# A two-layer hybrid backbone step: warm-up, early sum of squares and the last output in three parts

## The chip, the cores and the metric

The kernel runs on one core of a Trainium2 chip. The metric is the device time of one execution in microseconds (us), median of several runs.

The core has a matrix engine (TensorE, PE in the profile; its weight loads are listed as PEld), a vector engine (VectorE, DVE), a scalar engine (ScalarE, ACT), GpSimd (POOL) and a queue engine (SyncE, SP) that issues nearly all transfers here. TensorE's products land in PSUM, eight banks of 512 fp32 columns by 128 partitions.

## The reference

One inference step of two layers over 640 tokens (512 latent, 128 context) of width 1024. A layer does

```python
h = rms_norm(x, norm_g) * (1.0 + scale) + shift    # shift, scale, gate = silu(cond) @ ada_w[l] + ada_b[l]
u = h @ w_in[l]                                    # one wide input projection, cut into 16 parts
# four head groups on u: differential attention (A), gated convolution (B),
# latent attention (C), 2-D neighbourhood attention (D)
y = concat(group * silu(its gate path)) @ w_out[l]
x = x + gate * y
```

and a final RMSNorm with a gain follows the second layer. The modulation (`shift`, `scale`, `gate`) is one vector for the latent and one for the context tokens. The outputs are the final x and the context's keys and values of both layers. All arithmetic is fp32 accuracy: a large product is formed as three fp32r products of split operands (high x high, high x low, low x high).

## The kernel before

The activations stand transposed in the local memory, features on the 128 partitions, in eight feature blocks; tokens are columns, latent tokens 0 to 512, context 512 to 640. Every matrix operand is split into a high half, made by ScalarE as a rounded copy (`whi`, `hh`), and a low half, made by VectorE as the difference (`wlo`, `hl`).

The order of the work isn't the order of the code. The code records operations in a plan (`R`, an object of `Plan`), each with a priority: its place in the code, plus `R.offset`, plus a shift of its group from the table `SHIFT`. `Plan.schedule` then plays the machine through with prices from `Plan.price` and puts each engine's operations into one list; of those that can start, the one with the lowest priority goes first. In `Plan.price` an fp32r matmul costs 0.4375 ns for each moving column and 6 ns, and `schedule` lets one matmul start at the earliest 58 ns behind another (line 407). Each engine executes its list strictly in order. All operations are issued through one line of the program, so rows of the profile are told apart by tile names, not by lines.

The start of the kernel (lines 516 to 631, 847 to 875): the tokens of the first part (0 to 384, `START`) come by eight transfers into `cst`. The modulation weights of the first layer's first eight blocks come as 16 transfers of 512 KB (`adaw`), two for each block; `ada_first` multiplies each half by the condition vectors (`cs`), four matmuls that fill one PSUM bank in four strips, and derives `modB` and `modA`. The second part of the tokens (384 to 640) comes behind the fifth of these transfers (`X1`), and the four weight pieces of the first projection ("a") are put between them at the places of `WA`. `keep_warm` (line 544) lets TensorE multiply a matrix of ones by itself, 15 times ahead of everything and then 10, 8, 4 and 4 times behind the first four half blocks (`WARM`); these products are used by nobody. One fp32 matmul appears as two records in the trace. `rms_rows` (line 671) squares the eight feature blocks of a token part on ScalarE, adds them on VectorE, sums over partitions with one matmul by ones, and takes logarithm and exponential for the reciprocal root. `finish` (line 690) multiplies by the root, applies `modA` and `modB` and splits. Then the first projection runs (`tm_chunk`, 120 matmuls with 512 moving columns).

The end of a layer (lines 1313 to 1368): the output projection goes over token parts (`HALVES`), and within a part over eight feature blocks `fb`; a block is 24 matmuls (eight feature blocks, three products) with a 128 x 128 piece of `w_out` as the stationary operand and the part's tokens as the moving one. VectorE then adds gate times product to the old x (one instruction for latent and one for context tokens, where a part has both). Behind a part's eighth block, in the second layer, comes the final norm of that part: `rms_rows`, eight scalings by the gain, two multiplications by the root (each for four feature blocks) and two stores. The last part's sum of squares takes the eighth block in a matmul of its own (cuts 0, 7, 8). The second part's old x is fetched by one transfer into `xall`.

Of the kernel before, what the change touches and what calls it, by code (L numbers as in the profile page):

```python
# [20 lines left out]

L = 2
X1 = (4, 4, 4, 4, 4, 4, 4, 4)
WA = (2, 6, 11, 16)
LATE = (16, 17)
HALVES = (((0, 384), (384, 640)), ((0, 384), (384, 640)))
START = ((0, 384), (384, 640))
RMS = ((0, 8), (0, 8))
YK = (0, 1, 4, 5, 2, 6, 3, 7)
# [3 lines left out]
SWAP = 1290  # L33
SILU = 8
SLOW, LATER = 1.1, 800
WARM = (15, 10, 8, 4, 4)
SHIFT = {"": 38, "a0": 47, "a1": -28, "ada0": -8588, "av0": 6296, "av1": 3, "b0": 25951, "b1": 24557, "c0": -2462, "d0": 62, "d1": 33941, "f0.0": -174, "f0.1": 22, "f1.0": -183, "f1.1": 2841, "h0.0": -4317, "h0.1": 205, "h1.0": 7, "h1.1": -10499, "h10.0": 1418, "h10.1": -8, "h11.0": 638, "h11.1": 4686, "h2.0": -3351, "h2.1": -22079, "h3.0": -2855, "h4.0": -2974, "h4.1": -2909, "h5.0": -1, "h5.1": -9, "h6.0": 797, "h6.1": -6113, "h7.0": 20, "h7.1": 13278, "h8.0": 5300, "h9.0": -7596, "lam": 6901, "o0.0": -505, "o1.0": -80, "o1.1": 26, "p0.0": 162, "p0.1": -20, "p2.0": -2125, "p2.1": 432, "p3.0": -1337, "p3.1": 4371, "p4.0": -1388, "p4.1": -27369, "p7.0": -1727, "p7.1": 960, "p8.1": -18800, "pa0": 51, "pa1": -552, "qk00": -18970, "qk01": 10605, "qk10": 10903, "qk11": 14623, "x0": -3000, "x1": 6892, "x2": -1536, "y0": -1625, "y1": 9425, "y2": -77, "z0": -13, "z1": -227}
FILL = (('z', 4), ('d', 6), ('qk0', 7), ('qk1', 8), ('b', 12))
D = 1024
NT = 640  # L40
# [442 lines left out]
def body(ctx: ExitStack, tc: tile.TileContext, i, o):  # L483
# [12 lines left out]
    R = Plan()  # L496
    V, S, PE, SP = (R.engine(e) for e in ("DVE", "ACT", "PE", "SP"))

    def mmtile():
        return R.tile([128, 512], F32, tag="mm", space="psum")  # L500
# [41 lines left out]
    warm = mmtile()  # L542

    def keep_warm(n, after=None):
        for _ in range(n):
            PE.matmul(warm[:, 0:128], ones, ones, start=True, stop=True)
            if after is not None:
                R.ops[-1].deps.add(after)
                R.ops[-1].prio += 10 ** 6
                R.ops[-1].cost = {"PE": 215}  # L550
    keep_warm(WARM[0])
    for op in R.ops[-WARM[0]:]:
        op.cost = {"PE": 320}

    modA = R.tile([128, L, 8, 2], F32, name="modA")
    modB = R.tile([128, L, 8, 2], F32, name="modB")
# [1 line left out]
    b1 = R.tile([128, L, 8], F32, name="b1")  # L558
# [11 lines left out]
    def wpiece(l, name, idx):  # L570
        if l == 0 and name == "a":
            at(WA[idx])
            R.offset += WBOOST
        else:
            R.offset = 0
        off, kk, n = PIECES[name][idx]
        src = i["win"][l, off:off + 128 * kk * n].rearrange("(p c) -> p c", p=128)
        return wsplit(src, kk, n)

    def wsplit(src, kk, n, place=None):  # L580
        raw = R.tile([128, 1024], F32, name="wraw", tag="wraw", bufs=3)
# [13 lines left out]
    def at(h):  # L595

        R.offset = ada_at[min(h, 15)] + 7.5 * max(h - 15, 0) + 0.5 - len(R.ops)

    def ada_rows(l, blk, raws, warm):
        pa = (ttile if warm else mmtile)()  # L600
        for hf, raw in enumerate(raws):
            for k in range(4):
                PE.matmul(pa[32 * k:32 * k + 32, 0:256], cs[:, 4 * hf + k, :], raw[:, 256 * k:256 * k + 256],
                          start=(hf == 0), stop=(hf == 1))
            if warm and 2 * blk + hf < 4:
                keep_warm(WARM[1 + 2 * blk + hf], len(R.ops) - 1)
        sb = R.tile([128, 256], F32, name="adasb", bufs=1)
        S.activation(sb, pa[:, 0:256], AF.Copy)
        return sb

    def ada_first(l, blk, places):

        for hf in range(2):
            ada_at.append(len(R.ops))
            SP.dma_start(places[hf], i["adaw"][l, blk, hf])
        sb = ada_rows(l, blk, places, True)
        pb = ttile()
        for c in range(2):
            PE.matmul(pb[:, 2 * c:2 * c + 2], sb[:, 128 * c:128 * c + 128], sel, start=True, stop=True)
        R.need = len(R.ops) - 1  # L620
        V.tensor_scalar(modB[:, l, blk], pb[:, 0:2], sp[:, l, blk:blk + 1], None, op0=OP.add)
        V.tensor_scalar(modA[:, l, blk], pb[:, 2:4], b1[:, l, blk:blk + 1],
                        sp[:, l, 24 + blk:25 + blk], op0=OP.add, op1=OP.mult)

    def ada_block(l, blk):

# [209 lines left out]
    for l in range(L):  # L836
        if l == 0:
            flat = [(R.tile([128, 8, NT], F32, name="yt").rearrange("p a b -> p (a b)"), 5),
                    (R.tile([128, 6, 768], F32, name="adst").rearrange("p a b -> p (a b)"), 4),
                    (R.tile([128, 1280], F32, name="qs", bufs=2), 1),  # L840
                    (R.tile([128, 1280], F32, name="qs", bufs=2), 1),
                    (R.tile([128, 1536], F32, name="ks", bufs=2), 1),
                    (R.tile([128, 1536], F32, name="ks", bufs=2), 1),
                    (R.tile([128, BIAS_W], F32, name="bias"), 1),
                    (R.tile([128, 2816], F32, name="hl"), 2)]
            places = [t[:, 1024 * k:1024 * (k + 1)] for t, n in flat for k in range(n)]
            for blk in range(8):
                ada_first(0, blk, places[2 * blk:2 * blk + 2])
            R.need = None
            for kt in range(8):  # L850
                at(X1[kt])
                SP.dma_start(x_cur[1][:, kt], i["xt"][kt, :, START[0][1]:])
            R.begun = len(R.ops) - 1
            par = R.tile([128, P_W], F32, name="par")
            at(LATE[0])
            SP.dma_start(par, i["params"])
            ident, bones = par[:, 0:128], par[:, 128:256]
            rope = par[:, 256:512].rearrange("p (t c) -> p t c", t=4)
            fg = par[:, 512:520]
            lamt = R.tile([128, NT], F32, name="osb", bufs=2)[:, :L * 128].rearrange("p (l a c) -> p l a c", l=L, a=4)  # L860
            at(LATE[1])
            SP.dma_start(lamt, i["lam"].rearrange("l a c -> (l a c)").partition_broadcast(128)
                              .rearrange("p (l a c) -> p l a c", l=L, a=4))
            R.offset = 0
            rstds = []
            for n, x in enumerate(x_cur):
                R.group = f"x{n}"
                first = len(R.ops)
                rstds.append(rms_rows(x, RMS[n], n == 0))
                for op in R.ops[first:]:  # L870
                    op.deps.add(table)
            for kt in range(8):
                for n, (x, c, rstd) in enumerate(zip(x_cur, START, rstds)):
                    R.group = f"{'xy'[n]}{min(kt, 2)}"
                    finish(0, x, kt, *c, rstd)
            R.group = "lam"
            bonesr = R.tile([128, 128], F32R, name="bonesr")
            S.activation(bonesr, bones, AF.Copy)
            neglam = R.tile([128, L], F32, name="neglam")
            lprod = R.tile([128, NT], F32, name="osb", bufs=2)[:, :L * 64].rearrange("p (l a c) -> p l a c", l=L, a=2)  # L880
            for a in range(L):
                V.tensor_mul(lprod[:, a], lamt[:, a, 0:4:2, :], lamt[:, a, 1:4:2, :])
            V.tensor_reduce(lsum, lprod, AX.X, OP.add)
            S.activation(lsum, lsum, AF.Exp)
            V.tensor_sub(neglam, lsum[:, :, 1], lsum[:, :, 0])
            ga = R.tile([128, L], F32, name="ga")
            for a in range(L):
                li = 0.8 - 0.6 * math.exp(-0.3 * a)
                V.tensor_scalar(neglam[:, a:a + 1], neglam[:, a:a + 1], -li, None, op0=OP.add)
                V.tensor_scalar(ga[:, a:a + 1], sp[:, a, 32:33], 1.0 - li, None, op0=OP.mult)  # L890
            R.group = ""
# [425 lines left out]
        cstt = R.tile([128, 6 * C_W], F32, name="cst", tag="cst")  # L1317
        xns = halves(cstt, HALVES[l])
        wo = []
# [4 lines left out]
                    R.tile([128, 1024], F32R, name="wk", tag="ks", bufs=2)) for n in range(2)]  # L1324
        big2 = R.tile([128, 4, 1024], F32R, name="wyt", tag="yt")
        places += [(big2[:, 2 * n], big2[:, 2 * n + 1]) for n in range(2)]
        c0, c1 = HALVES[l][1]
        xall = R.tile([128, 2816], F32, name="xall", tag="hl")[:, :8 * (c1 - c0)].rearrange("p (k c) -> p k c", k=8)
        SP.dma_start(xall, xsrc[:, :, c0:c1].rearrange("k p c -> p k c"))
        for hf, (c0, c1) in enumerate(HALVES[l]):  # L1330
            R.group = f"o{hf}.{l}"
            xn = xns[hf]
            for fb in range(8):
# [3 lines left out]
                wh, wl = wo[fb]  # L1337
                w = c1 - c0
                if hf:
                    xo = xall[:, fb]  # L1340
                else:
                    xo = R.tile([128, NT], F32, name="xo", tag=("osb", "q3")[fb % 2], bufs=(2, 4)[fb % 2])
                    SP.dma_start(xo[:, :w], xsrc[fb, :, c0:c1])
# [11 lines left out]
                if l + 1 < L:  # L1355
                    SP.dma_start(xdram[fb, :, c0:c1], xn[:, fb])
            R.group = f"f{hf}.{l}"
            rstd = rms_rows(xn, (0, 7, 8) if l + 1 == L and hf == 1 else (0, 8))
            if l + 1 < L:
                for kt in range(8):  # L1360
                    finish(l + 1, xn, kt, c0, c1, rstd)
# [123 lines left out]
```

## Time and profile before

| | us |
|---|---|
| median of 3 runs | 825.73 (825.54 to 825.94) |
| the profiled execution | 825.87 |
| its span, first to last instruction | 824.1 |
| TensorE listed busy | 799.7 (97%) |
| VectorE | 578.9 (70%) |
| ScalarE | 505.0 (61%) |

The page lists an engine as busy from the start of an instruction to its end; the ends of matmuls are modelled and overlap with the next one's start, so the spacing of starts tells what a matmul costs, and a stretch without idle time isn't a stretch at the peak. A row of the timeline joins neighbouring instructions of one form: start, length from the first start to the last end, engine, operation, tiles, shape and count; what stands in brackets is the idle time before it and what ended it. The granted clock of TensorE has two levels here, 1.0 (2.4 GHz) and 0.5 (1.2 GHz); a stretch with both shows a value between.

### The profile page before, as it was taken

To read this page: it belongs to the slowest core of one execution; us is meant where nothing else is said; L and a number is where in the kernel's file an instruction comes from. 1 tells how busy PE (TensorE), PEld (TensorE's weight loads), DVE (VectorE), ACT (ScalarE), POOL (GpSimd) and SP (SyncE) were. 2 spreads that over 40 slices of the span, in tenths; PEclk is the share of its full clock that TensorE was granted. 3 is DMA by queue.
4 is the path that set the end of the run, shared out by engine and by line. 5 is a ranking of instruction groups with operands and counts; after the bars stand their busy time and mean duration, and the time that the engine had idled before them with its cause. 6 is when DMAs were issued, how large, how long until landed. Compare 5 with 4: busy or idle time off the path is not lost.

```text
span 824.1 us, 14974 instructions
## 1 busy us (share of the span) xinstructions
PE 799.7 (97%) x5570; PEld 746.0 (91%) x5570; DVE 578.9 (70%) x1296; ACT 505.0 (61%) x1108; POOL 0.2 (0%) x4
## 2 busy tenths in 40 slices
PE   7999999998999999999999999999999999999995
PEld 6789898998898888989998899999999989999995
DVE  3744499798674985837367636986987899876643
ACT  5852487677883874624237436866887878645432
POOL 0000000000000000000000000000000000000000
PEclk8999999999999999999999999999999999999998
DMA  9924533444562787756650355333146646823221
GB/s 313 364 100 109 169 88 83 114 133 119 173 162 83 186 259 203 254 170 215 238 193 30 89 139 165 105 79 104 61 108 159 145 106 184 254 70 90 84 77 52
DMA packets 50029, 120.15 MB, mean 146 GB/s; under 512 B 7940, under 2 KB 21892, under 8 KB 49956
## 3 DMA queue, kind: packets, MB, share of 16 engines
q1 hardware_dynamic: 49812, 119.11, 48.2%
q8 instruction: 44, 0.72, 0.4%
q14 instruction: 29, 0.24, 0.1%
q10 hardware_dynamic: 144, 0.07, 0.0%
HBM read 82.69 MB, written 6.59 MB: 108 GB/s over the span
## 4 chain that ended last, share of the span: by engine, by line
PE 85%; ACT 5%; DVE 4%; DMA 3%; issue 1%; SPq 1%; DVEq 0%; ACTq 0%
PE bank L464 81%; PE pair L464 5%; ACT t L464 2%; ACT thi L464 1%; DVE t L464 1%; DMA wraw<-adaw 1%; DMA bias<-bias 1%; DVE tlo L464 1%; DMA yt<-adaw 1%; SPq L464 1%; DVE mn L464 1%; DMA q<-hl 0%; DVE cst L464 0%; ACT avt L464 0%; DVE adasb L464 0%
## 5 line engine op out<-in xcount | busy, mean ns | idle before, releaser
L464 PE MATMUL bank<-hh,whi 128*128 128x320 f32 (+2 forms) x640 | 202.2, 317 | 0.3 <-ACT adasb L464 0.3
L464 PE MATMUL bank<-hh,wlo 128*128 128x320 f32 (+2 forms) x640 | 201.0, 315 | 0.0
L464 PE MATMUL bank<-hl,whi 128*128 128x320 f32 (+2 forms) x640 | 200.7, 314 | 0.0
L464 PEld LDWEIGHTS bank<-hh,whi 128*128 128x128 f32 x640 | 120.5, 188 | 2.8 <-issue 1.2
L464 PEld LDWEIGHTS bank<-hh,wlo 128*128 128x128 f32 x640 | 120.3, 188 | 2.4 <-issue 1.6
L464 PEld LDWEIGHTS bank<-hl,whi 128*128 128x128 f32 x640 | 120.6, 188 | 2.1 <-issue 1.2
L464 DVE TENSOR_TENSOR wlo<-wraw,whi 128x1024 fp32r<-128x1024 f32 (+1 forms) x64 | 76.5, 1195 | 62.8 <-ACT whi L464 62.5
L464 ACT ACTIVATE thi<-bank 128x512 fp32r<-128x512 f32 (+3 forms) x164 | 76.8, 486 | 49.1 <-PE bank L464 45.4
L464 PE MATMUL bank<-whi,hl 128*128 128x256 f32 (+2 forms) x320 | 105.9, 332 | 0.0
L464 PE MATMUL bank<-whi,hh 128*128 128x256 f32 (+2 forms) x320 | 105.1, 333 | 0.7 <-DVE adst L464 0.5
L464 PE MATMUL bank<-wlo,hh 128*128 128x256 f32 (+2 forms) x320 | 105.1, 329 | 0.0
L464 DVE TENSOR_TENSOR tlo<-bank,thi 128x512 fp32r<-128x512 f32 (+3 forms) x164 | 86.8, 548 | 16.9 <-ACT thi L464 16.1
L464 ACT ACTIVATE whi<-wraw 128x1024 fp32r<-128x1024 f32 (+1 forms) x64 | 66.3, 1035 | 51.9 <-PE bank L464 40.6
L464 DVE TENSOR_REDUCE mn<-pair 128x1 f32<-128x640 f32 x96 | 77.9, 816 | 7.0 <-PE pair L464 4.4
L464 ACT ACTIVATE t<-pair,mn 128x640 f32<-128x640 f32 x96 | 75.9, 792 | 9.2 <-DVE mn L464 6.1
L464 PE MATMUL bank<-par,t 128*128 128x128 f32 x456 | 79.6, 274 | 1.4 <-DVE tlo L464 1.4
L464 PE MATMUL pair<-ks,qs 96*128 96x320 f32 (+1 forms) x256 | 62.9, 327 | 4.6 <-ACT t L464 4.3
L464 PEld LDWEIGHTS bank<-whi,hh 128*128 128x128 f32 x320 | 60.1, 189 | 6.6 <-issue 0.8
L464 PE MATMUL bank<-thi,vs 128*128 128x256 f32 (+3 forms) x224 | 64.3, 295 | 0.8 <-ACT t L464 0.8
L464 PEld LDWEIGHTS bank<-whi,hl 128*128 128x128 f32 x320 | 60.3, 188 | 5.1 <-issue 1.6
L464 PEld LDWEIGHTS bank<-wlo,hh 128*128 128x128 f32 x320 | 60.4, 189 | 5.0 <-issue 1.2
L464 PE MATMUL bank<-tlo,vs 128*128 128x256 f32 (+3 forms) x224 | 64.0, 303 | 0.5 <-DVE tlo L464 0.5
(191 smaller groups left out, 1450.7 us busy)
## 6 DMA issues: line engine op xcount, KB each, us to landing
wraw<-win SPq DMA_DIRECT2D x52, 512.0 KB, 4.1
wraw<-adaw SPq DMA_DIRECT2D x32, 512.0 KB, 4.8
ks<-hl SPq DMA_DIRECT2D x48, 192.0 KB, 3.6
wraw<-wout SPq DMA_DIRECT2D x16, 512.0 KB, 3.9
bias<-bias SPq DMA_DIRECT2D x8, 896.0 KB, 6.8
ks<-hl SPq DMA_DIRECT2D x48, 96.0 KB, 2.2
qs<-hl SPq DMA_DIRECT2D x48, 80.0 KB, 2.1
qs<-hl SPq DMA_DIRECT2D x24, 160.0 KB, 2.5
```

The lines of the kernel that those rows point to most:

```text
L464: done = getattr(engines[op.engine], method)(*[fix(x) for x in args], **{k: fix(x) for k, x in kw.items()})
```

## The change

`WARM` goes from 15, 10, 8, 4, 4 to 34, 4, 4, 4, 4, and the planner's price of the first ones is set to 340 ns for 14 and 215 ns for the rest. `WA` moves the four weight pieces of the first projection to earlier places among the modulation transfers, from behind the 4th, 8th, 12th and 16th of them to behind the 2nd, 6th, 12th and 16th, as the places and shifts work out. The matmul that sums the first token part's squares is made a condition of the four matmuls of the second half of modulation block 0 (`second`), and the split of the first weight piece is made to wait for that part's root (`R.rooted`). `modB` and `modA` of the first blocks get a better priority. In the second layer the output projection goes over three token parts, 0 to 384, 384 to 512 and 512 to 640; `xall` is still fetched as one. `SHIFT` is a new table.

```diff
-WA = (2, 6, 11, 16)
+WA = (0, 5, 10, 15)
 LATE = (16, 17)
-HALVES = (((0, 384), (384, 640)), ((0, 384), (384, 640)))
+HALVES = (((0, 384), (384, 640)), ((0, 384), (384, 512), (512, 640)))
...
-WARM = (15, 10, 8, 4, 4)
-SHIFT = {"": 38, "a0": 47, "a1": -28, "ada0": -8588, ...}
+WARM = (34, 4, 4, 4, 4)
+SHIFT = {"": 38, "a0": 44, "a1": -74, "ada0": -10517, ...}
...
     keep_warm(WARM[0])
-    for op in R.ops[-WARM[0]:]:
-        op.cost = {"PE": 320}
+    for n, op in enumerate(R.ops[-WARM[0]:]):
+        op.cost = {"PE": 340 if n < 14 else 215}
...
-        return wsplit(src, kk, n)
+        split_at = len(R.ops) + 1
+        w = wsplit(src, kk, n)
+        if l == 0 and name == "a" and idx == 0:
+            R.ops[split_at].deps.add(R.rooted)
+        return w
...
+    second = []
+
     def ada_rows(l, blk, raws, warm):
         pa = (ttile if warm else mmtile)()
         for hf, raw in enumerate(raws):
+            if warm and blk == 0:
+                second.append(len(R.ops))
...
         V.tensor_scalar(modA[:, l, blk], pb[:, 2:4], b1[:, l, blk:blk + 1],
                         sp[:, l, 24 + blk:25 + blk], op0=OP.add, op1=OP.mult)
+        for op in R.ops[-2:]:
+            op.prio -= 3000
...
                 rstds.append(rms_rows(x, RMS[n], n == 0))
+                if n == 0:
+                    R.rooted = len(R.ops) - 1
                 for op in R.ops[first:]:
                     op.deps.add(table)
+                    if n == 0 and "PE" in op.calls:
+                        for k in range(4):
+                            R.ops[second[1] + k].deps.add(op.n)
...
-        c0, c1 = HALVES[l][1]
+        c0, c1 = HALVES[l][1][0], NT
...
-                    xo = xall[:, fb]
+                    xo = xall[:, fb, c0 - HALVES[l][1][0]:c1 - HALVES[l][1][0]]
...
-            rstd = rms_rows(xn, (0, 7, 8) if l + 1 == L and hf == 1 else (0, 8))
+            rstd = rms_rows(xn, (0, 7, 8) if l + 1 == L and hf == 2 else (0, 8))
```

## Rows read from the trace of the kernel before

**Rows 1.** Part 1 of the page: busy time of each engine.
```profile
PE 799.7 (97%) x5570; PEld 746.0 (91%) x5570; DVE 578.9 (70%) x1296; ACT 505.0 (61%) x1108; POOL 0.2 (0%) x4
```

**Rows 2.** The chain of waits, its longest piece: start, length, what.
```profile
677.60 136.54 PE bank L464 x938
```

**Rows 3.** Stretches of the start: length, busy of each engine, clock, DMA share, GB/s.
```profile
9.00:10.00 1.00, 0.00 (x0) 0.00 (x0) 0.90 (x2) 0.00 (x0) 0.00 (x0) 0.67 1.01 381
...
15.00:16.00 1.00, 1.00 (x4) 0.70 (x5) 0.00 (x0) 0.26 (x1) 0.00 (x0) 0.50 1.01 391
...
20.82:31.28 10.46, 10.46 (x83) 1.00 1.00 397
31.28:61.88 30.60, 30.60 (x186) 1.00 0.50 174
```

**Rows 4.** Timeline of the start, TensorE.
```profile
1.05 5.93 PE L464 MATMUL bank<-ones 128*128 128x128 f32 x30 [1.05 <-DVE ones L464]
...
10.71 1.08 PE L464 MATMUL bank<-yt,cs 128*32 128x256 f32 x8 [3.74 <-DMA yt<-adaw]
...
15.33 1.23 PE L464 MATMUL bank<-t,ones 128*128 128x384 f32 x2
...
23.01 2.17 PE L464 MATMUL bank<-ones 128*128 128x128 f32 x18
...
30.71 0.64 PE L464 MATMUL bank<-adst,cs 128*32 128x256 f32 x8
```

**Rows 5.** Timeline of the start, VectorE: additions of the first sum of squares.
```profile
6.30 4.54 DVE L464 TENSOR_TENSOR t<-t,t 128x384 f32<-128x384 f32 x7 [2.36 <-ACT t L464]
```

**Rows 6.** Timeline of the start, VectorE and ScalarE ahead of 31.28 us.
```profile
30.20 1.21 DVE L464 TENSOR_TENSOR wlo<-wraw,whi 128x1024 fp32r<-128x1024 f32 x1
...
30.60 0.47 ACT L464 ACTIVATE thi<-bank,epst 128x256 f32<-128x256 f32 x1 [0.66 <-PE bank L464]
```

**Rows 7.** Timeline of the start, issues on SP's queue.
```profile
17.38 1.38 SPq L464 DMA_DIRECT2D adst<-adaw  x3
...
18.80 0.43 SPq L464 DMA_DIRECT2D wraw<-win  x1
```

**Rows 8.** The last token part's matmuls: length, TensorE busy, clock, DMA share, GB/s.
```profile
790.54:813.97 23.43, 23.43 (x195) 1.00 0.19 69
```

**Rows 9.** Timeline of TensorE around a single 128-column matmul.
```profile
352.55 0.22 PE L464 MATMUL bank<-thi,vs 128*128 128x128 f32 x1
352.60 0.36 PE L464 MATMUL bank<-hh,wlo 128*128 128x320 f32 x1
352.80 0.31 PE L464 MATMUL bank<-hh,whi 128*128 128x320 f32 x1
352.95 0.31 PE L464 MATMUL bank<-hl,whi 128*128 128x320 f32 x1
```

**Rows 10.** Timeline of TensorE, four 128-column matmuls in a row.
```profile
340.59 0.44 PE L464 MATMUL bank<-ks,qs 128*128 128x128 f32 x2
340.86 0.28 PE L464 MATMUL bank<-thi,vs 128*128 128x128 f32 x1
340.98 0.27 PE L464 MATMUL bank<-tlo,vs 128*128 128x128 f32 x1
341.09 0.36 PE L464 MATMUL bank<-hh,wlo 128*128 128x320 f32 x1
```

**Rows 11.** Timeline of the tail: add, sum, root, multiplications, store issues.
```profile
814.17 0.61 DVE L464 SCALAR_TENSOR_TENSOR cst<-bank,modG,hl 128x128 f32<-128x128 f32 x2 [1.29 <-PE bank L464]
...
815.28 0.70 PE L464 MATMUL bank<-tlo,ones 128*128 128x256 f32 x2 [0.72 <-ACT tlo L464]
816.02 0.47 ACT L464 ACTIVATE thi<-bank,epst 128x256 f32<-128x256 f32 x1 [0.25 <-PE bank L464]
...
816.97 2.36 DVE L464 TENSOR_TENSOR cst<-cst,thi 128x1024 f32<-128x1024 f32 x2 [2.19 <-ACT thi L464]
818.23 1.55 SPq L464 DMA_DIRECT2D yt<-cst  x2
```

More of the change, by code (lines that the diff above doesn't have):

```diff
@@ L35 @@
 SLOW, LATER = 1.1, 800
-WARM = (15, 10, 8, 4, 4)
-SHIFT = {"": 38, "a0": 47, "a1": -28, "ada0": -8588, "av0": 6296, "av1": 3, "b0": 25951, "b1": 24557, "c0": -2462, "d0": 62, "d1": 33941, "f0.0": -174, "f0.1": 22, "f1.0": -183, "f1.1": 2841, "h0.0": -4317, "h0.1": 205, "h1.0": 7, "h1.1": -10499, "h10.0": 1418, "h10.1": -8, "h11.0": 638, "h11.1": 4686, "h2.0": -3351, "h2.1": -22079, "h3.0": -2855, "h4.0": -2974, "h4.1": -2909, "h5.0": -1, "h5.1": -9, "h6.0": 797, "h6.1": -6113, "h7.0": 20, "h7.1": 13278, "h8.0": 5300, "h9.0": -7596, "lam": 6901, "o0.0": -505, "o1.0": -80, "o1.1": 26, "p0.0": 162, "p0.1": -20, "p2.0": -2125, "p2.1": 432, "p3.0": -1337, "p3.1": 4371, "p4.0": -1388, "p4.1": -27369, "p7.0": -1727, "p7.1": 960, "p8.1": -18800, "pa0": 51, "pa1": -552, "qk00": -18970, "qk01": 10605, "qk10": 10903, "qk11": 14623, "x0": -3000, "x1": 6892, "x2": -1536, "y0": -1625, "y1": 9425, "y2": -77, "z0": -13, "z1": -227}
+WARM = (34, 4, 4, 4, 4)
+SHIFT = {"": 38, "a0": 44, "a1": -74, "ada0": -10517, "av0": 16444, "b0": 19703, "b1": 26350, "c0": -3769, "c1": 49, "d0": -5, "d1": 38767, "f0.0": -2204, "f0.1": -5582, "f1.0": -285, "f1.1": -6126, "f2.1": 4916, "h0.0": -8657, "h0.1": 159, "h1.0": -15, "h1.1": -10538, "h10.0": 973, "h10.1": 5197, "h11.0": 902, "h11.1": -5190, "h2.0": -7936, "h2.1": -14771, "h3.0": -2883, "h3.1": -5905, "h4.0": -3198, "h4.1": -1914, "h5.0": 26, "h5.1": -219, "h6.0": 539, "h6.1": -6063, "h7.0": -1651, "h7.1": 9503, "h8.0": 10455, "h9.0": -6876, "h9.1": 9608, "lam": 6420, "o0.0": -423, "o0.1": -71, "o1.1": 37, "o2.1": 133, "p0.0": -2458, "p0.1": -20, "p2.0": -2664, "p2.1": 431, "p3.0": -1437, "p3.1": 4287, "p7.0": -1937, "p7.1": 126, "p8.0": 1182, "p8.1": -17028, "pa0": -17, "pa1": -9314, "qk00": -12230, "qk01": 11804, "qk10": 11705, "qk11": 14512, "x0": 2128, "x1": 639, "x2": -3103, "y0": -5212, "y1": 3068, "y2": -19754, "z0": -21, "z1": -227}
 FILL = (('z', 4), ('d', 6), ('qk0', 7), ('qk1', 8), ('b', 12))
```

## The prediction

> **What bounds the kernel now.** I read the page first: TensorE is listed busy for 799.7 of 824.1 us [rows 1], so the idle time that any reordering could remove is 24.4 us. The chain of waits says the same of the end: from 677.60 us on it is one unbroken run of TensorE matmuls, 136.54 us long, up to the last output [rows 2]. So what is added to TensorE there comes out at the end one to one. Then I read the three stretches that the change touches.
>
> The start. TensorE runs 15 warm-up matmuls (30 records) from 1.05 us to 6.98, then has nothing until the first modulation weights arrive: 3.74 us idle before 10.71 [rows 4]. In that gap the granted clock falls (0.67 on average in 9 to 10 us) and in 15 to 16 us it is still 0.50, which is 1.2 of 2.4 GHz [rows 3]. At that clock a half block of eight modulation records takes 1.08 us; at the full clock, 0.64 [rows 4]. The DMA queues are full at the same time (share 1.00 in 20.82 to 31.28 us). From 31.28 us the DMA share is 0.50 and TensorE works without a gap [rows 3]. The 31.28 us have two reasons that end together: the low half of the second weight piece of the first projection, made from 30.20 to 31.41 us, and the reciprocal root for the second token part, whose logarithm starts at 30.60 [rows 6].
>
> The last part, tokens 384 to 640: 192 matmuls of 256 columns. With one sum of squares in between (2 to 3 records) they take 23.43 us [rows 8]. I take 0.6 us off for that sum: 22.8 us, 0.119 us for each.
>
> The tail, behind the last of these: add the residual, square, sum over partitions, logarithm, exponential, multiply, store. It runs from 814.17 us to 824.1 [rows 11], with all TensorE work done by 815.98.
>
> **The last output in three token parts.** The 256 columns become two times 128, so 192 matmuls become 384, each with a weight load of its own. If time went by columns alone, that would cost nothing. The trace has 128-column matmuls in fp32r, in ones to fours, and their record reads wrongly at first sight. At 352.55 us one starts and its successor starts 0.05 us later; but that successor, a 320-column one, lasts 0.36 us where its like take 0.31, and the next starts 0.20 us behind it instead of the usual 0.15 [rows 9]. The two together took 0.25 us; less the 0.15 of the 320 columns, 0.10 us are left for 128 columns. In a row it shows directly: from 340.86 us two 128-column matmuls and the start of the next stand 0.12 and 0.11 us apart [rows 10], 0.115 each. I read this as the weight load: with 128 columns the matmul is shorter than the load of the following weights, and 256 columns (0.119) just cover it. The low end is the 0.05 of the recorded start, the high end 0.115; I take 0.11, since it is what two different neighbourhoods give once the delay of the successor is counted. Then 384 x 0.11 = 42.2 us in place of 22.8: +19.4 us (from +0.2 at 0.06, to +21.4 at 0.115). One more sum of squares adds two records and a change of form, 0.3 us. Together +19.7 us, all of it on the run of [rows 2]. Nothing hides it: the work beside it on VectorE and ScalarE grows by eight squares, seven additions, a root and two multiplications, which have 2.6 us for each feature block and don't set the pace.
>
> The Trainium skill ("TensorE: Matmul & The Clock Gate", section "Back-to-back issue gap") gives about 81 ns as the sustained spacing of weight load and matmul at 128 columns; by it the sum for this part, as an estimate, would be 384 x 0.081 - 22.8 + 0.3 = +8.6 us. The rows above are longer than that, and the measured ones are kept.
>
> **The shorter tail.** With 128 columns in place of 256: one residual addition after the last matmul, not two in 0.61 us (-0.3); the sum of squares 0.70 us, of it two records at half the columns (-0.2); square, logarithm and exponential (-0.1 each); the first of two multiplications, 2.36 us for both, ends after half the time (-0.6) [rows 11]. The two stores move half as much. They are issued from 818.23 us on, and 5.9 us later the span ends [rows 11]; I take -1.0 for them, between -0.3 (a fixed delay) and -1.5 (half of the 3 us in which they move data, as an estimate from 1.05 MB). Sum -2.4 us (-1.7 to -2.9).
>
> **The start.** The new warm-up has 34 matmuls, 68 records. The first 30 took 5.93 us; the other 38 at the full clock, 0.12 us each (18 such records take 2.17 us from 23.01 us on [rows 4]), need 4.6 us and end at about 11.5, some 0.7 us beyond the arrival of the first weights at 10.71. That closes the gap in which the clock falls. Behind it 16 warm-up matmuls are left in place of 26. The first sum of squares, whose additions end at 10.84 us [rows 5] but which is executed at 15.33 [rows 4] because both halves of block 0 and ten warm-up records stood ahead of it, now goes ahead of the second half. What that costs: the second half's four matmuls wait for the sum, and whatever is queued on TensorE behind them waits too, about 0.7 us of sum and only if its adds were late, which they aren't. On SP's queue the first weight piece passes two modulation transfers, and the second piece (issued 18.80, behind three that start at 17.38 [rows 7]) passes two; the same bytes must come, so each passed transfer lands some 1.3 us later (512 KB at the 397 GB/s of [rows 3]).
>
> What is it worth? Not the time of the fillers that go, since TensorE ran them while it waited. The date that counts is 31.28 us. The second piece lands two transfers earlier, 2.6 us; the first root comes some 4 us earlier and takes the first token part's work off ScalarE and VectorE before the second part's squares arrive. So both releasers move by 2.6 to 4 us. I take -3.5 us, between 0 (the x transfers of the second part, which the change leaves where they are, set the date) and -6.5.
>
> **The new order table.** It moves work of both layers; no row prices an order. Of the 24.4 us idle, 4.8 stand at the start (1.05 and 3.74), 8.8 in the tail (8.1, and 0.72 before the last sum), so 10.8 us lie between. Ends: -8 (most of this goes) and +8 (as much again comes). I take 0.
>
> **Sum.** The profiled execution took 825.87 us (span 824.1, 1.8 around it), 0.14 above the median of 825.73. 825.9 + 19.7 - 2.4 - 3.5 + 0 = 839.7 us.
>
> **Rivals.**
> A (faster): the weight loads of the 128-column stream are hidden after all, as the recorded start 0.05 us behind suggests [rows 9]. The price is then 384 x 0.06 = 23.0, so +0.2 + 0.3; 825.9 + 0.5 - 5.9 = 820.5 us. It decides as soon as a matmul costs under about 0.075 us (384 x 0.075 + 0.3 - 22.8 = 6.3, what start and tail give). Against it: no run of two or more in the trace keeps that pace, which is why it gets 10%.
> B: half of the load is hidden, 0.085 us each: 32.6 - 22.8 + 0.3 = +10.1, and 830.0 us. The rows of this trace are dearer, 5%. The Trainium skill's 81 ns from the section named above stands close to this price.
> C: the transfers set the date in the start, which gives nothing, and the order loses 5 us: 825.9 + 19.7 - 2.4 + 5 = 848.2 us. For it speaks a DMA share of 1.00 up to 31 us. 9%.
> D: start and order both reach their good ends: 825.9 + 19.7 - 2.4 - 6.5 - 8 = 828.7 us. 10%.
> E: the longer warm-up doesn't do what it says, because the second wait for weights, after 11 us, lets the clock fall once more. Then the modulation records of the first two blocks cost 0.44 us more for each eight, 1.8 us in all: 841.5 us. 8%.
> The forecast has the other 58%, with 834 to 845 as its own range.
>
> **Range and chances.** A difference under 0.2% (824.1 to 827.4 us) can't be told from none in this kernel. The range of 827 to 847 takes in B, D, E and the forecast and leaves out A, most of C and the edge of D. Faster: A, 10%. Same: 2%, from the edge of D. Slower: 88%.
>
> **What would show it.** Right: in the last two token parts matmuls of 128 columns stand 0.11 us apart on average, some 42 us for 384, in an unbroken run; the tail is near 7.5 us; no fall of the granted clock between 9 and 16 us; the first projection ends before 59 us, not at 61.88, where the last window of [rows 3] ends. Wrong: about 24 us for the 384 matmuls (A), or a first projection that ends no earlier (C). The forecast falls if the 128-column runs, longer than any that the trace holds, behave unlike the ones, twos and fours.

## The result, and the profile after

The changed kernel takes 839.28 us (median of 4 runs, 838.71 to 840.56), the kernel before, measured beside it, 825.63: 1.0171 times as long, 95% interval 1.0153 to 1.0188. The profiled execution took 839.09 us with a span of 837.1. The forecast was 839.7 us. Runs of the kernel before differ with the clock: beside the experiments below, nine of them with a mean granted clock of 0.995 took 823.6 us on average, six with 0.992 took 826.1.

TensorE's part of the page and the longest piece of the chain of waits, answering [rows 1] and [rows 2]:

```profile
PE 819.1 (98%) x5782; PEld 766.4 (92%) x5782; DVE 579.8 (69%) x1302; ACT 510.0 (61%) x1129; POOL 0.2 (0%) x4
```

```profile
715.84 113.80 PE bank L464 x831
```

TensorE has 212 more records and is listed busy 19.4 us longer: 192 of the new ones are matmuls of the last output, 18 are warm-up, 2 the additional sum of squares. The end is still one unbroken run of TensorE.

The start: stretches as in [rows 3] (length, busy time of PE, PEld, DVE, ACT and POOL, clock, DMA share, GB/s), then its timeline for TensorE as in [rows 4], for VectorE and ScalarE as in [rows 6], and for SP's queue as in [rows 7]:

```profile
9.00:10.00 1.00, 1.00 (x11) 1.00 (x10) 0.83 (x2) 0.23 (x1) 0.00 (x0) 1.00 0.87 332
15.00:16.00 1.00, 1.00 (x17) 0.88 (x15) 0.50 (x2) 1.00 (x3) 0.00 (x0) 1.00 1.02 384
...
28.33:58.35 30.02, 30.02 (x184) 22.55 (x183) 16.36 (x44) 20.51 (x47) 0.00 (x0) 1.00 0.60 222
```

```profile
1.04 10.68 PE L464 MATMUL bank<-ones 128*128 128x128 f32 x68 [1.04 <-DVE ones L464]
11.66 0.64 PE L464 MATMUL bank<-yt,cs 128*32 128x256 f32 x8
...
13.22 0.81 PE L464 MATMUL bank<-t,ones 128*128 128x384 f32 x2
```

```profile
25.33 1.23 DVE L464 TENSOR_TENSOR wlo<-wraw,whi 128x1024 fp32r<-128x1024 f32 x1
25.92 0.46 ACT L464 ACTIVATE thi<-bank,epst 128x256 f32<-128x256 f32 x1
```

```profile
18.36 0.43 SPq L464 DMA_DIRECT2D wraw<-win  x1
```

The clock no longer falls, the eight modulation records take 0.64 us instead of 1.08, the first sum of squares stands at 13.22 us instead of 15.33, and both releasers of the dense stretch come 4.7 to 4.9 us earlier. The first projection ends at 58.35 us instead of 61.88.

The last two token parts, as a stretch against [rows 8], and the beginning of its timeline:

```profile
785.76:829.46 43.70, 43.70 (x389) 1.00 0.15 49
```

```profile
785.76 0.22 PE L464 MATMUL bank<-hh,whi 128*128 128x128 f32 x1
785.83 0.27 PE L464 MATMUL bank<-hl,whi 128*128 128x128 f32 x1
785.93 0.28 PE L464 MATMUL bank<-hh,wlo 128*128 128x128 f32 x1
786.05 0.28 PE L464 MATMUL bank<-hh,whi 128*128 128x128 f32 x1
786.16 0.28 PE L464 MATMUL bank<-hl,whi 128*128 128x128 f32 x1
```

The first two starts are 0.07 us apart, as behind the single matmul of [rows 9]; from the second on they stand 0.10 to 0.12 apart, and the median over all 384 is 0.112 us. The part takes 43.70 us in place of 23.43.

The tail, as in [rows 11]:

```profile
829.66 0.35 DVE L464 SCALAR_TENSOR_TENSOR cst<-bank,modG,hl 128x128 f32<-128x128 f32 x1 [1.66 <-PE bank L464]
...
830.41 0.49 PE L464 MATMUL bank<-tlo,ones 128*128 128x128 f32 x2 [0.51 <-ACT tlo L464]
830.94 0.37 ACT L464 ACTIVATE thi<-bank,epst 128x128 f32<-128x128 f32 x1
...
831.68 1.29 DVE L464 TENSOR_TENSOR cst<-cst,thi 128x512 f32<-128x512 f32 x2 [1.66 <-ACT thi L464]
832.39 1.01 SPq L464 DMA_DIRECT2D yt<-cst  x2
```

From the end of the last part to the end of the span it is 7.7 us (829.46 to 837.1) in place of 10.1 (813.97 to 824.1).

So the 13.1 us of the span are: first projection 3.5 us earlier; another 1.3 us gained between it and the last part, which starts at 785.76 instead of 790.54; last part +20.3; tail -2.4.

### The profile page after: what moved, and what is told of

Its sections match the earlier page's. It is cut to its first block, busy times and chain, and to the rows that moved or that the text cites. A ratio compares the mean times of both kernels' runs of the same rounds, so it can differ in the third digit from the quotient of the medians.

```text
span 837.1 us, 15419 instructions
## 1 busy us (share of the span) xinstructions
PE 819.1 (98%) x5782; PEld 766.4 (92%) x5782; DVE 579.8 (69%) x1302; ACT 510.0 (61%) x1129; POOL 0.2 (0%) x4
## 4 chain that ended last, share of the span: by engine, by line
PE 82%; DVE 6%; DMA 5%; ACT 4%; issue 1%; SPq 1%; DVEq 0%; ACTq 0%
PE bank L464 78%; PE pair L464 4%; DMA wraw<-adaw 2%; ACT t L464 2%; DVE t L464 2%; ACT thi L464 1%; SPq L464 1%; DMA bias<-bias 1%; DVE tlo L464 1%; DVE mn L464 1%; DVE wlo L464 1%; ACT avt L464 0%; ACT whi L464 0%; DMA q<-hl 0%; DMA wraw<-wuq 0%
## 5 line engine op out<-in xcount | busy, mean ns | idle before, releaser
L464 PE MATMUL bank<-hh,whi 128*128 128x320 f32 (+3 forms) x656 | 205.9, 315 | 0.7 <-ACT adasb L464 0.5
L464 PE MATMUL bank<-hh,wlo 128*128 128x320 f32 (+3 forms) x656 | 205.7, 315 | 0.0
L464 PE MATMUL bank<-hl,whi 128*128 128x320 f32 (+3 forms) x656 | 205.4, 314 | 0.0
L464 PEld LDWEIGHTS bank<-hh,whi 128*128 128x128 f32 x656 | 123.7, 189 | 3.4 <-issue 1.2
L464 PEld LDWEIGHTS bank<-hh,wlo 128*128 128x128 f32 x656 | 123.5, 189 | 2.4 <-issue 1.6
L464 PEld LDWEIGHTS bank<-hl,whi 128*128 128x128 f32 x656 | 123.8, 189 | 1.9 <-issue 1.2
```

Of the source, the lines that this page charges most:

```text
L464: done = getattr(engines[op.engine], method)(*[fix(x) for x in args], **{k: fix(x) for k, x in kw.items()})
```

## The experiments

In all of them the clock is at its full level in the last output unless something else is said.

**The loss alone, both ways.** First the changed kernel with the two old token parts (e1; later expectations call the kernels by such numbers); all lists of all engines are the same as in the changed kernel up to the last stage.

```diff
-HALVES = (((0, 384), (384, 640)), ((0, 384), (384, 512), (512, 640)))
+HALVES = (((0, 384), (384, 640)), ((0, 384), (384, 640)))
...
-            rstd = rms_rows(xn, (0, 7, 8) if l + 1 == L and hf == 2 else (0, 8))
+            rstd = rms_rows(xn, (0, 7, 8) if l + 1 == L and hf == 1 else (0, 8))
```

> The changed kernel with the old two token parts in the last output; start, order table and all else as changed. Theory (the third part costs TensorE 20.3 us and gives 2.4 us back in the tail): the last part starts at 785.8 us as in the changed kernel, takes 23.4 us and has a tail of 10.1 us, span 819.3, time 821.3 us, so 0.5% faster than the kernel before. Rival (the new order table, not the three parts, carries the loss): at or above 835 us.

Measured: 820.84 us (820.43 to 822.07), 0.9959 of the kernel before, interval 0.9944 to 0.9974. The last part again takes 23.65 us, two records of a sum of squares more than in [rows 8] among them:

```profile
785.33:808.98 23.65, 23.65 (x197) 1.00 0.19 67
```

The tail is 9.6 us, not the 10.1 expected. Up to the first store's issue it runs as in [rows 11]; from the end of the last issue to the end of the span it is 3.8 us, where the kernel before had 4.3 with the same stores, so executions differ by that much.

The rival is out: start and order are a gain, the three parts alone turn it into a loss, by some 18 us (18.4 between the medians, 17.5 by the two ratios).

Then the reverse, the kernel before with the three token parts and nothing else (e2; `HALVES`, `xall` and the cuts as in the diff of the change).

> The kernel before with the three token parts alone; old warm-up, old places, old order table. Theory: 825.6 + 20.3 - 2.4 = 843.5 us, with the 384 matmuls of 128 columns 0.111 us apart. Rival (the loss comes from the start or the order): 823 to 826 us.

Measured: 846.48 us (845.73 to 847.16), ratio 1.0267, interval 1.0249 to 1.0284. The 384 matmuls stand 0.112 us apart and take 43.5 us, as forecast, but the time is 3 us too long. The timeline of the tail shows where:

```profile
833.06 0.44 PE L464 MATMUL bank<-thi,ones 128*128 128x128 f32 x2
...
834.34 0.68 DVE L464 TENSOR_TENSOR cst<-cst,thi 128x512 f32<-128x512 f32 x1
...
837.27 0.79 PE L464 MATMUL bank<-thi,ones 128*128 128x128 f32 x2 [3.78 <-DVE thi L464]
837.86 0.63 PE L464 MATMUL bank<-tlo,ones 128*128 128x128 f32 x2
...
839.27 1.29 DVE L464 TENSOR_TENSOR cst<-cst,thi 128x512 f32<-128x512 f32 x2 [2.05 <-ACT thi L464]
```

Two sums of squares stand behind the last matmul. The one at 833.06 belongs to the second token part, whose finish the old table puts last; the third part's squares and additions share ScalarE and VectorE with it, and TensorE waits 3.78 us for them. The tail is 11.6 us long (833.06 to 844.6). So the third part shortens the tail only if the second one's finish stands among the third's matmuls. This was tested with four shifts of the new table (e10; the rest of the old table kept):

```diff
-"f1.1": 2841, ... "o1.1": 26,
+"f1.1": -6126, "f2.1": 4916, ... "o1.1": 37, "o2.1": 133,
```

> As e2 (the kernel before with three token parts), but with the shifts of the groups o1.1, o2.1, f1.1 and f2.1 from the new table; only the last stage's lists change, and the second part's root now stands among the third part's matmuls. Theory (e2's tail of 11.5 us holds the second part's whole finish, because the old table shifts it late): tail 7.7 us, time 3.9 us below e2, 842.6 us. Rival (three parts crowd the tail in any order): within 1 us of e2's 846.5.

Measured: 841.85 us (841.35 to 842.59). The sum of the second part is gone from the tail:

```profile
832.96 0.49 PE L464 MATMUL bank<-tlo,ones 128*128 128x128 f32 x2 [0.51 <-ACT tlo L464]
...
834.23 1.29 DVE L464 TENSOR_TENSOR cst<-cst,thi 128x512 f32<-128x512 f32 x2 [1.66 <-ACT thi L464]
```

The span ends at 839.6, 7.6 us behind the last matmul. Of the 4.6 us between the two kernels, 4.0 are this tail.

**What the 0.112 us are.** Two theories give the same price for 128 columns: the load of the next weights, which a short matmul doesn't cover, and a half rate for narrow moving operands. Two kernels part them. In the first (e3) the last two parts are 192 and 64 columns wide:

```diff
-HALVES = (((0, 384), (384, 640)), ((0, 384), (384, 512), (512, 640)))
+HALVES = (((0, 384), (384, 640)), ((0, 384), (384, 576), (576, 640)))
```

> The changed kernel with the last two token parts cut as 192 and 64 columns in place of 128 and 128. Theory 1 (each matmul waits for the load of the next 128 x 128 weights, whatever its columns): both widths stand 0.11 us apart, 192 x 0.22 = 42.6 us for both parts. Theory 2 (fp32r matmuls under 256 columns stream at half rate, two clocks for a column): 192 columns 0.165 us apart, 64 columns 0.058, together 42.8 us. The sum is the same, the two spacings tell them apart. The whole time is about 838 to 840 us by both.

The timeline of the 192-column part, then of the 64-column part:

```profile
784.55 0.27 PE L464 MATMUL bank<-hh,wlo 128*128 128x192 f32 x1
784.66 0.27 PE L464 MATMUL bank<-hh,whi 128*128 128x192 f32 x1
...
811.14 0.28 PE L464 MATMUL bank<-hl,whi 128*128 128x64 f32 x1
811.25 0.28 PE L464 MATMUL bank<-hh,wlo 128*128 128x64 f32 x1
```

Both stand 0.11 us apart (median 0.112 in each), three times as many columns or not: theory 1. The whole time, however, was 851.32 us (one run), 12 us above both forecasts. The stretches of the two parts (length, TensorE busy, clock, DMA share, GB/s):

```profile
784.35:806.41 22.06, 22.06 (x195) 1.00 0.20 72
806.41:812.33 5.92, 5.92 (x55) 1.00 0.00 0
812.33:842.50 30.17, 30.17 (x144) 0.50 0.09 27
```

After 5.9 us of 64-column matmuls the granted clock fell to 1.2 GHz and stayed there, although TensorE never stood idle. At that level they stand 0.21 us apart, twice as far.

In the second kernel (e8) the moving 128 columns stay and the stationary operand is halved in the last two parts, which leaves out half of the output features there (the old x stands in their place):

```diff
-                    PE.matmul(acc[:, :w], wh[:, kt], hh[kt][:, c0:c1], start=(n == 0), stop=False)
+                    PE.matmul(acc[0:fw, :w], wh[:, kt, 0:fw], hh[kt][:, c0:c1], start=(n == 0), stop=False)
...
+                        if half:
+                            V.tensor_copy(xn[64:128, fb, d0 - c0:d1 - c0], xo[64:128, d0 - c0:d1 - c0])
```

> The changed kernel, but in the last two token parts the stationary operand has 64 of its 128 columns, so half of the output features of these parts are left out (the old x is copied there); the moving 128 columns stay. Theory 1 (weight load, in proportion to the stationary columns): about 0.06 us apart, 23 to 24 us for both parts, time about 820 us. Theory 2 (half rate for narrow moving operands): still 0.111 us apart, 43 us, time about 839 us. A load time that doesn't depend on the stationary columns would also give 0.111.

Measured: 819.32 us (one run). The stretch of both parts and its timeline:

```profile
785.11:809.20 24.09, 24.09 (x390) 1.00 0.27 88
```

```profile
785.29 0.22 PE L464 MATMUL bank<-hh,whi 128*64 128x128 f32 x1
785.35 0.22 PE L464 MATMUL bank<-hl,whi 128*64 128x128 f32 x1
785.41 0.22 PE L464 MATMUL bank<-hh,wlo 128*64 128x128 f32 x1
```

With half of the stationary columns the same moving operand takes 0.06 us. The half rate is out, and the price falls with the stationary columns. The size of the output isn't the cause: 64 moving columns halve it too, and there the price stayed. Strict proportion isn't shown, because 0.06 us is also about half the price of a 256-column matmul (0.119), so the load of 64 columns may be shorter still. The Trainium skill ("TensorE: Matmul & The Clock Gate", section "LDWEIGHTS (loading the stationary operand)") gives the load as columns divided by 1.2 GHz, for 128 columns 107 ns as an estimate; the 0.112 us here are close to it at the full clock, the 0.21 us at the half clock are twice as long, and there the measurement decides. The 81 ns of the Trainium skill (same page, section "Back-to-back issue gap") for the sustained spacing at 128 columns don't hold for these fp32r operands: 0.112 us was measured.

**The start.** Two kernels change the warm-up and leave every engine's list in its order. In one (e4), 19 of the 34 matmuls of the two-part kernel above aren't issued; in the other (e5), 19 are added to the kernel before, behind its first 15.

```diff
     keep_warm(WARM[0])
+    R.dropped = {op.n for op in R.ops[-19:]}
...
         for op in self.schedule():
+            if op.n in self.dropped:
+                continue
```

> As e1 (changed kernel, two token parts), with every engine's list in the same order, but 19 of the first 34 warm-up matmuls are not issued; nothing else moves. If the clock matters for the start: the granted clock falls to 0.50 about 9 to 16 us, the modulation records and the first sum there cost some 1 to 1.8 us more, and the time is 1 to 2 us above e1 (822 to 823). If the transfers set the date of the first projection all the same: within 0.5 us of e1, or even 0.3 us less, because the weights that arrive at 10.7 us no longer wait for the end of the warm-up at 11.7.

Measured: 821.80 us (821.16 to 822.96), 0.9963 of the kernel before (0.9949 to 0.9977): 1.0 us above the 820.84, with intervals that overlap. The first projection ends 0.6 us later in the profile. The clock fell, but for a shorter time than in the kernel before (granted 0.50 from 10.5 to 13.9 us; there 9.3 to 16.2), so this measures only part of it:

```profile
10.50:11.50 1.00, 0.55 (x8) 0.50 0.97 397
12.00:13.00 1.00, 1.00 (x8) 0.50 1.02 418
15.00:16.00 1.00, 1.00 (x16) 1.00 1.03 383
```

```diff
             op.name = done.ins.name
+            if op.n == self.lengthen:
+                for _ in range(19):
+                    getattr(engines[op.engine], method)(*[fix(x) for x in args], **{k: fix(x) for k, x in kw.items()})
```

> The kernel before, with every engine's list in the same order and 19 more warm-up matmuls behind the first 15; nothing else moves. If the half clock alone cost the start: no fall of the clock, the first projection ends 1 to 2 us earlier and the time is 824 to 825 us. If the date of 31.28 us is set by the second weight piece and the second root, which the longer warm-up leaves where they are: first projection at 61.9 us as before, time 825.6 us within 0.5.

Measured: 823.62 us (823.21 to 826.19), ratio 0.9985, interval 0.9974 to 0.9996. TensorE's timeline and the two releasers of [rows 6]:

```profile
5.92 4.41 PE L468 MATMUL bank<-ones 128*128 128x128 f32 x38
10.28 0.64 PE L464 MATMUL bank<-yt,cs 128*32 128x256 f32 x8
...
18.39 0.97 PE L464 MATMUL bank<-whi,hh 128*128 128x512 f32 x3
```

```profile
27.75 1.21 DVE L464 TENSOR_TENSOR wlo<-wraw,whi 128x1024 fp32r<-128x1024 f32 x1
28.15 0.47 ACT L464 ACTIVATE thi<-bank,epst 128x256 f32<-128x256 f32 x1 [0.65 <-PE bank L464]
```

With the warm-up alone both releasers come 2.45 us earlier, and the first projection ends at 59.40 us instead of 61.88. So the date of 31.28 us wasn't set by the transfers, but by TensorE, whose records at half clock (fillers among them) held up the roots and splits of the other engines. Of the 2.5 us, 0.4 stand already at the first modulation records of this execution (10.28 against 10.71). The 2.5 us are also the upper end: e2 and e10 have the old start in the same order, and there the first projection ended at 61.39 and 60.90 us, so the gain is 1.5 to 2.5 us by the profiles, and 1.2 us (0.3 to 2.1) by the ratio of the times.

The other two parts of the start were undone one at a time in the two-part kernel. The planner makes a new list then, so each result holds that too. First the condition of the early sum (e11):

```diff
-                            R.ops[second[1] + k].deps.add(op.n)
+                            pass
```

> As e1 without the condition that puts the first sum of squares ahead of the second half of modulation block 0; the planner then puts it behind that half and one warm-up matmul, and replans what follows. Theory (the long warm-up gave 2.5 us of the start's 3.5, the early sum and the places the rest): first projection ends 0.3 to 1 us later than 58.4 us, time 821 to 822. Rival (the early root is what starts the projection earlier): 2 us or more later, time above 822.5.

Measured: 821.37 us (820.61 to 822.03), first projection at 58.4 us. The sum starts at 13.70 us here, 0.5 us later than in the changed kernel and still well ahead of the 15.33 of the kernel before, so this takes back the condition and not the whole of the sum's move.

Then the places of the weight pieces (e6):

```diff
-WA = (0, 5, 10, 15)
+WA = (2, 6, 11, 16)
```

> As e1 with the first projection's four weight pieces at the old places among the modulation transfers (behind the 4th, 8th, 12th and 16th); the planner replans what follows. If the places are worth the rest of the start: first projection ends 0.5 to 1 us later than 58.4 us, time 821.3 to 822. If the transfers' order sets the start, 2 us or more later; if TensorE sets it, no later.

Measured: 820.85 us (819.71 to 821.39), first projection at 58.5 us. Neither the early sum nor the places move the projection by themselves: 58.4 us with both. The two releasers of [rows 6] did move with the places:

```profile
27.71 0.47 ACT L464 ACTIVATE thi<-bank,epst 128x256 f32<-128x256 f32 x1
...
28.29 1.21 DVE L464 TENSOR_TENSOR wlo<-wraw,whi 128x1024 fp32r<-128x1024 f32 x1
```

They come 1.8 and 3.0 us later than in the changed kernel, and the projection ends within 0.1 us of it. So these two don't set its date.

**The order table.** The two-part kernel with the old table (e7).

```diff
-SHIFT = {"": 38, "a0": 44, "a1": -74, "ada0": -10517, ...}
+SHIFT = {"": 38, "a0": 47, "a1": -28, "ada0": -8588, ...}
```

> As e1 with the old order table; the planner makes a new list from it, so all stretches move a little. If the new table is worth the 1.3 us that stand between the first projection and the last part, the time is about 822.6 us; if the old table fits the new start badly, 824 to 830; if the table is worth nothing by itself, 821.

Measured: 822.24 us (819.90 to 823.27), ratio 0.9966 (0.9951 to 0.9981). The spread covers the 820.84 of the new table. In the profile the stretch from the end of the first projection to the last token part isn't longer than with the new one, so the 1.3 us gained there aren't shown to be the table's. The first projection, however, ends at 59.6 us instead of 58.4, although both releasers come earlier than with the new table (24.66 and 25.26 us): TensorE stands idle for 1.7 us in that start, most of it in one place.

```profile
36.58 0.64 PE L464 MATMUL bank<-ks,cs 128*32 128x256 f32 x8 [1.52 <-DMA ks<-adaw]
```

In this execution the old order makes TensorE wait for a modulation transfer. About 1 us of the start is thus a matter of the table; one execution shows it, and the times don't tell the two apart.

**A shorter tail without narrow matmuls.** The two-part kernel (e9) with the last part's final multiplication and store in four pieces.

```diff
-                for k in (0, 4):
-                    y = xn[:, k:k + 4]
+                m = 2 if hf else 4
+                for k in range(0, 8, m):
+                    y = xn[:, k:k + m]
```

> As e1 (two token parts), but the last part's final multiplication and store are made in four pieces of two feature blocks, not two of four. The first store can be issued after 0.6 us of multiplication, not 1.2, so the tail should shorten by 0.4 to 0.7 us: 820.7 us against 821.3 for e1. Rival: four issues of some 0.8 us on one queue eat that, same time as e1 or 0.5 us more.

Measured: 820.78 us (819.83 to 821.60), no different from 820.84. The timeline of the two-part kernel, then of this one:

```profile
811.98 2.36 DVE L464 TENSOR_TENSOR cst<-cst,thi 128x1024 f32<-128x1024 f32 x2 [2.19 <-ACT thi L464]
813.23 1.55 SPq L464 DMA_DIRECT2D yt<-cst  x2
```

```profile
813.10 2.50 DVE L464 TENSOR_TENSOR cst<-cst,thi 128x512 f32<-128x512 f32 x4 [2.19 <-ACT thi L464]
813.82 2.21 SPq L464 DMA_DIRECT2D yt<-cst  x4
```

The first store is issued 0.72 us behind the start of the multiplications instead of 1.25, but the last one no sooner: its issue ends 2.93 us behind that start instead of 2.80. From there to the end of the span it is 3.8 us in both. What counts here is the last issue, and behind it a time that didn't shrink with the size of the last store (512 KB there, 256 KB here; the kernel before had 4.3 us with 512 KB).

## Why the prediction was right

**The last part.** Forecast +19.7 us with the sum, measured +20.3. The mechanism was read from single matmuls and fours [rows 9, 10]: the successor's delay belongs to the price of the short one. The spacing is 0.112 instead of 0.11, which makes 0.8 us over 384, and that covers the difference of 0.6. That the cause is the weight load, only argued there, is now shown by the two kernels with 192 and 64 moving and with 64 stationary columns. Rivals A and B fall with the 0.112.

**The tail.** Forecast -2.4 us, measured -2.4. The terms come out too: the multiplications start 0.78 us sooner behind the last matmul (forecast 0.8), the first store is issued 0.55 us sooner behind their start (0.6), and from there the span ends 1.07 us sooner (1.0). Some of this last term is luck: about 0.5 us of it stands behind the last issue, where the kernel before and e1 differ by 0.4 with the same stores, and against e1 the tail is only 2.0 us shorter. One condition wasn't seen: the second part's finish must not stand in the tail. The new table saw to that; with the old one the gain is a loss of 1.5 us.

**The start.** Forecast -3.5 us, measured -3.5, but the reason given was wrong, and the agreement is luck. The step that failed is "not the time of the fillers that go, since TensorE ran them while it waited", with the second weight piece's earlier transfer and the early root as movers. TensorE didn't wait. From the first modulation record to the end of the first projection it is listed without idle time in both kernels (length, TensorE busy, clock, DMA share, GB/s; the kernel before, then the changed one):

```profile
10.71:61.88 51.17, 51.17 (x337) 0.95 0.70 260
11.66:58.35 46.69, 46.69 (x317) 1.00 0.74 276
```

So the date is the sum of what TensorE's records cost, and the 4.5 us between the two stretches are worked out from these: 2.2 us of half clock (0.88 for 16 modulation records, 0.9 for eight fillers, 0.4 for the first sum) and 20 filler records fewer, 2.2 us at 0.112. The later first record, 11.66 us against 10.71, takes 0.95 of it back. The half clock was tested (e5, 1.5 to 2.5 us); the 20 fillers weren't taken out alone, so their share is a count from the traces. The two releasers named did move, by more than forecast (4.7 to 4.9 us), but e6 and e7 move them either way without the projection following. Rival C, transfers that set the date and leave the start no gain, is out; e7 shows that they stand close behind. The overhang of the warm-up is longer than the 0.7 us forecast, because its records stand 0.213 us apart until 7.0 us here, until 5.9 in the kernel before and until 4.1 in e5, and 0.112 from then on. E is out too: the clock stays.

**The order.** Forecast 0, measured -1.3 between the first projection and the last part. The old lists took 728.7, 728.2 and 727.4 us for this stretch in three executions (the kernel before, e2, e10) and the changed kernel 727.4, so the 1.3 us are within what executions differ by, and the table's gain isn't shown there; e7 puts about 1 us of it into the start. With the other terms, -3.5 - 1.3 + 20.3 - 2.4 = +13.1 against +13.8. The total is as near as it is partly because the 0.6 us that the last part costs more and the 1.3 us gained here have opposite signs.

The version that beats both is the changed kernel with two token parts (e1): 820.84 us, 0.4% below the kernel before.

## What to carry to other kernels

Price a matmul by the later of its moving columns and the load of the next stationary operand. In fp32r with 128 x 128 weights 64, 128 and 192 moving columns all cost 0.112 us here and 256 cost 0.119, so cutting below 256 columns saved almost nothing for each matmul and doubled their number. In a trace read the price from a pair, the short one and the delay of its successor, not from the gap to the next start. A finer last part shortens a tail only when the finish of the part before has left it. And before calling a wait the date of a stage, look whether TensorE is idle ahead of it: if it isn't, its own records are the date, fillers included.

## What was not expected of the hardware

A stream of 64-column matmuls without listed idle time lost the full clock after 5.9 us and ran on at 1.2 GHz, at 0.21 us each (one execution); in the streams of 192 and 128 columns at the same 0.11 us spacing (22 and 43.7 us long) the clock stayed. The price that the weight load sets doubles with the halved clock: 0.112 to 0.21 us. And the length of the half-clock stretch in the start isn't fixed for one and the same list of TensorE: 9.3 to 16.2 us in the kernel before, 8.6 to 15.5 in e2 and 11.8 to 15.3 in e10, whose lists for the start are the same and where the first projection ended at 61.4 and 60.9 us instead of 61.88.
